# Side products of a three-layer block emitted in batches with a least distance, feeding of operands excepted

## The chip, the cores and the metric

One core of one Trainium2 chip runs the whole program. The metric is the device time of one execution in microseconds; before the change it is 2408.99 us, the median of three runs (2408.96 to 2410.69).

## What is computed

Two blocks follow each other on a sequence of 256 tokens of width 2048, all in float32. The first has two layers of the same form (cut):

```python
h = x @ w_in                                       # split into 11 parts
y_a = chunk_band_attention(a_q, a_k, a_v, table)   # 8 heads of 128, chunks of 64
o_b = gla_chunk_recurrence(b_q, b_k, b_v, log_g)   # 4 heads, gated linear attention, normed
y_m = memory_attention(m_q, *split(mem @ w_mem_kv))  # 4 heads
y = concat([y_a * silu(a_z), y_b * silu(b_z), y_m * silu(m_z)])
x = layer_norm(ALPHA * x + y @ w_out)
```

The second block has one layer:

```python
proj = rms_norm(x) @ w_in                          # a_q a_f a_i a_g b_q b_k b_v b_f g_a g_b
y_a = hgrn2_mixer(a_q, a_f, a_i, a_g) @ w_up_a     # 8 heads: gated recurrence over chunks of 64
y_b = fox_mixer(b_q, b_k, b_v, b_f) @ w_up_b       # 8 heads: causal softmax with decays
x = x + rms_norm((sigmoid(g_a) * y_a + sigmoid(g_b) * y_b) @ w_o)
gate, up = split(rms_norm(x) @ w_ffn_in)           # 5632 each
x = x + rms_norm((silu(gate) * up) @ w_ffn_down)
```

## The kernel before

Nearly all of TensorE's time goes into the large products with the weight matrices. They are a list of jobs, in the order in which they run (`run`, line 212). A job makes 512 output columns (or two jobs of 256, where the output is wanted with features on the partitions) over all rows of the weight; its weight comes in tiles of 128 x 1024 numbers. Each number is split into a high and a low part in the reduced float type that TensorE multiplies fast: ScalarE casts the high part (line 271) and VectorE subtracts it (line 272), and three matmuls (lines 329 to 331) or two (lines 338 and 339) use the parts. One tile is a unit. Its loads (SP's queue) and splits are emitted ahead, up to six split tiles and four raw ones, as far as the 41 slots of SBUF that all stages share allow (`ahead`, `room`). When a job's last unit is emitted, its `post` reads the result out of PSUM.

The small products (scores, transposes, read-outs of attention and recurrence heads, transposes of operands) are side work. A head is a Python generator that emits some instructions, yields a delay and is continued later. A planner keeps a clock in nanoseconds: a unit adds 2623, a side product 1.69 per column. A generator is due when its delay has passed on that clock. After each unit `pump` (line 194) continues the two that have been due longest. A bank is one of four PSUM buffers of 512 columns for side products (`bank`). Tokens allow three recurrence heads and three attention heads at a time. `drain` (line 199) continues given generators until they end, whatever their delay; a `post` or a read of an operand calls it where it needs the result.

Nothing is reordered later: each engine runs its instructions in the order in which they were emitted.

The generators that matter here:

- `hgrn_head` (line 751), one for each of 8 heads in the second block, and for each of two halves t of the sequence: `decay_levels` (line 666: eleven GpSimd instructions, then Abs and Exp of 128 x 1024 on ScalarE, lines 684 and 685), delay 10000; fifteen multiplies on GpSimd (lines 765 to 771), 7500; score products of four levels into one bank and a masked read-out on VectorE (line 781), 3500; the same for four more levels, 3500; for the second half the product with the first half's keys (the cross product), a sum over levels on VectorE (line 784), 5500; the read-out into a bank, its squares on ScalarE (line 691), the power on GpSimd (line 446) and the scaling on VectorE (line 693), 9000; a transpose, 0.
- `banded` (line 602), the softmax heads of both blocks (f heads in the second): scores, bias and maximum on VectorE, exponentials on ScalarE (line 615), scaling on VectorE (line 618), 7000; transposes and a copy by ScalarE (line 623), 8000; the product with the values.
- `post_f` (line 1229), the post of the gate columns f0 and f1, each in two halves: a copy by ScalarE (line 471), two passes of VectorE (lines 472 and 483), two sigmoids (lines 1237 and 1238), three passes of GpSimd (lines 1242 to 1244).
- `post_ag` (line 1339), the post of the output gate's columns: its first half drains the four recurrence heads of the group, and both halves end in a GpSimd multiply (line 812).
- `feeder` and `late_feed` (lines 457 and 529), which transpose and split the operand of the next jobs.

Of the kernel before, what the change touches and what calls it, by code (L numbers as in the profile page):

```python
# [32 lines left out]
NEAR = 8  # L33
HOLD = 4
N_WARM = 12


L0 = 11000
L1 = 7000
F0 = 4500  # L40
F1 = 5500
FG = 1250
# [54 lines left out]
class Builder:  # L97
    def __init__(self, ctx, tc, a):
        self.tc, self.nc, self.a = tc, tc.nc, a
        pool = lambda name, bufs, **kw: ctx.enter_context(tc.tile_pool(name=name, bufs=bufs, **kw))  # L100
        self.const = pool("const", 1)
        self.tmp = pool("tmp", 2)
        self.small = pool("small", 4)
        self.psm = pool("psm", 2, space=bass.MemoryType.PSUM)
        self.pss = pool("pss", 4, space=bass.MemoryType.PSUM)
        self.dram = pool("dram", 1, space=bass.MemoryType.DRAM)
        self.free = list(range(N_SLOT))
        self.act = self.const.tile([P, NKT, 2, S], F32R, tag="act", name="act")
        self.slots = [self.const.tile([P, 1024], F32, tag=f"slot{i}", name=f"slot_{i}") for i in range(N_SLOT)]
        self.side, self.ready, self.pending = [], {}, []  # L110
        self.tokens = {"att": N_ATT, "lin": N_LIN}
        self.clock = 0.0
        self.n = 0


# [28 lines left out]
        return self.tmp.tile(shape, F32, tag=tag, name=self.name(tag), bufs=bufs)  # L144

    def bank(self):
        return self.pss.tile([P, 512], F32, tag="bank", name=self.name("bank"))

    def load(self, out, in_):
        self.nc.sync.dma_start(out, in_)  # L150


    def start(self, gen):
        self.side.append(gen)
        self.ready[gen] = self.clock

    def later(self, fn, delay=1500):
# [34 lines left out]
        self.tokens[kind] -= 1  # L192

    def pump(self):
        due = [g for g in self.side if self.ready[g] <= self.clock]
        for gen in sorted(due, key=lambda g: self.ready[g])[:2]:
            self.step(gen)

    def drain(self, gens):
        tries = 0  # L200
# [179 lines left out]
def network(ctx, tc, a):  # L380
    B = Builder(ctx, tc, a)
# [75 lines left out]
    def feeder(act, t, delay, gap=1500):  # L457
        yield delay
        while act.left[t]:
            act.feed_next(t)  # L460
            yield gap
# [97 lines left out]
    late = {}  # L559

    def start_late(act, *args):
        late["gen"] = late_feed(act, *args)
        B.start(late["gen"])

    def need_rows(act):

# [254 lines left out]
    def memory_jobs(l, act, pre_v=None, pre_k=None, after=None):  # L821
        jobs.append(Job("x", a["w_mem_kv"][l], 512, 512, act, keep_x(mv, l), pre=pre_v))
        wjobs(a["w_mem_kv"][l], 0, act, keep(mk, l, then=after), pre=pre_k)
# [19 lines left out]

    def start_x():
        load_x()
        B.start(first_x())

    def first_x():
        yield 8000
        x_head["ids"] = B.alloc(2, F32R)  # L850
        slot_split(x_head["ids"], v4(x_in[0]))
        B.release([x_in.pop(0)])

    mem_act = Act(main_get, feed_mem, quads, both=True)

    def mem_start():
        load_mem(1)

        def rest():
            for c in (2, 3):  # L860
                load_mem(c)
                mem_act.feed_next(0)
                yield 2000
            B.load(ident, a["c_ident"])
            mem_act.feed_next(0)
        B.start(rest())

    (mem_in[0],) = B.alloc(1)
    mem_act.left[0].pop(0)
# [7 lines left out]
    (load_a, split_a), (load_b, split_b) = mem_half(0), mem_half(1)  # L877
    load_a()
    split_a()
    memory_jobs(0, mem_act, mem_start, start_x, lambda: B.start(feeder(x0, 0, 0)))  # L880

    def head_get(ids):

# [33 lines left out]
    def layer(l, act, head):  # L917
# [126 lines left out]
        def early():  # L1044
            B.release(head())
            for _ in range(3):
                yact.feed_next(0)
            B.start(feeder(yact, 0, 1000))

        W(3584, act, post_z(1, "A1", early), pre=y_head)  # L1050

# [27 lines left out]
        def finish(t):  # L1079
# [7 lines left out]
            if l == 0:  # L1087
                def norm():
                    xsrc["ids"] = st["r"]
                    yield L0 * t  # L1090
                    for c in range(4):
                        V.scalar_tensor_tensor(rows(c), rows(c), mvt[:, 0:1], st["g"](c), ALU.subtract, ALU.mult)
                        V.scalar_tensor_tensor(rows(c), rows(c), rs[:, 0:1], st["bb"](c), ALU.mult, ALU.add)
                    for c in range(4):
                        nc.gpsimd.dma_start(xres[t * P:(t + 1) * P, c * 512:(c + 1) * 512], rows(c))
                    yield from feeder(nact, t, L1)
                    if t == 1:
                        B.release(st["gi"] + st["bi"] + st["head"])
                B.start(norm())
                return  # L1100


# [18 lines left out]

            st[t] = rows, center, stretch, shift
            if t == 0:
                B.start(feeder(nact, 0, F0, FG))
                return

            B.release(st["gi"] + st["wi"])
# [363 lines left out]
    def mix_done(ids, t):  # L1491
        if t == 0:
            xsrc["ids"] = B.alloc(4)

        def rows(c):
            return vt(ids[c])[:, t, :]

        for c in range(4):
            eng = V if c % 2 == 0 else G
            eng.tensor_tensor(vt(xsrc["ids"][c])[:, t, :], rows(c), f["wb"](c), ALU.mult)  # L1500

        f[t] = rows
        if t == 0:
            B.start(feeder(fact, 0, F0, FG))
        else:
            start_late(fact, [f[0], f[1]], x1res, None, lambda: B.release(ids + f["wi"]), False)

# [138 lines left out]
```

## Time and profile before

| | |
|---|---|
| median of 3 runs | 2408.99 us (2408.96 to 2410.69) |
| the profiled execution | 2409.21 us, of it span 2407.4 us |
| mean granted clock of TensorE | 0.998 |
| TensorE busy (matmuls) | 2391.0 us, 99%, 12105 matmuls |
| VectorE busy | 1471.4 us, 61% |
| ScalarE busy | 1098.7 us, 46% |
| GpSimd busy | 399.6 us, 17% |
| DMA | 464.65 MB, mean 193 GB/s |

PE is TensorE's matmuls, PEld its weight loads, DVE VectorE, ACT ScalarE, POOL GpSimd, SP the engine that issues most DMAs. Matmuls are pipelined: the time of one in a row is longer than the distance to the next, so distances of starts are to be read, not durations.

### The profile page before, as it was taken

What the parts mean: (1) busy time and instruction counts of PE and PEld (TensorE: products, weight loads), DVE (VectorE), ACT (ScalarE), POOL (GpSimd) and SP (SyncE); (2) the same over time, 40 slices, a digit from 0 to 9 for tenths busy, and PEclk for the clock granted to TensorE, in tenths of its full rate; (3) what the DMA queues carried; (4) which work ended last, traced back from release to release, by engine and by line L of the source; (5) the groups of instructions that cost most, each with busy time, mean ns of one, the idle gap of its engine ahead of it and who ended that gap; (6) DMA issues with size and microseconds to landing.
All of it is one profiled execution on the core that took longest, in us unless ns stands there. A gap on an engine that the chain in (4) does not pass through costs nothing.

```text
span 2407.4 us, 31457 instructions
## 1 busy us (share of the span) xinstructions
PE 2391.0 (99%) x12105; PEld 2015.4 (84%) x12105; DVE 1471.4 (61%) x1671; ACT 1098.7 (46%) x1472; POOL 399.6 (17%) x601
## 2 busy tenths in 40 slices
PE   9999999999999999999999999999999999999998
PEld 7888888888888888888888888887888888888886
DVE  6587557666855667766675656657545544554455
ACT  5444445345454553555545444445434423443333
POOL 0330010004400110364654430001000000000000
PEclk9999999999999999999999999999999999999999
DMA  9646567674656674954554666675755655555653
GB/s 325 186 149 184 171 188 262 207 241 133 186 159 188 205 258 154 279 166 124 178 164 143 200 190 193 201 243 180 243 176 181 194 184 192 203 182 177 208 193 131
DMA packets 313911, 464.65 MB, mean 193 GB/s; under 512 B 21960, under 2 KB 161568, under 8 KB 313760
## 3 DMA queue, kind: packets, MB, share of 16 engines
q1 hardware_dynamic: 312528, 459.48, 60.3%
q8 instruction: 95, 1.56, 0.3%
q0 software_dynamic: 640, 2.10, 0.2%
q10 hardware_dynamic: 592, 1.06, 0.1%
q14 instruction: 56, 0.46, 0.1%
HBM read 454.18 MB, written 8.40 MB: 192 GB/s over the span
## 4 chain that ended last, share of the span: by engine, by line
PE 91%; issue 6%; DVE 1%; ACT 0%; DMA 0%; POOL 0%; SPq 0%; DVEq 0%; POOLq 0%
PE main_j L338 19%; PE main_j L329 19%; PE main_j L330 19%; PE main_j L331 19%; PE main_j L339 10%; PE bank L372 4%; PE bank L376 1%; PE main_j L334 0%; DMA slot<-in_memT_dram 0%; DVE slot L1480 0%; DVE slot L272 0%; SPq L150 0%; POOL slot L673 0%; ACT slot L271 0%; POOL slot L812 0%
## 5 line engine op out<-in xcount | busy, mean ns | idle before, releaser
L272 DVE TENSOR_TENSOR slot<-slot,slot 128x1024 fp32r<-128x1024 f32 x810 | 1003.0, 1284 | 200.2 <-ACT slot L271 196.5
L271 ACT CAST slot<-slot 128x1024 fp32r<-128x1024 f32 x810 | 807.5, 1047 | 254.9 <-DVE slot L272 129.0
L338 PE MATMUL main_j<-act,slot 128*128 128x512 f32 x1824 | 651.3, 400 | 0.0
L329 PE MATMUL main_j<-slot,act 128*128 128x512 f32 x1608 | 635.6, 395 | 0.6 <-ACT slot L271 0.6
L330 PE MATMUL main_j<-slot,act 128*128 128x512 f32 x1608 | 626.5, 390 | 1.4 <-DVE slot L272 1.2
L331 PE MATMUL main_j<-slot,act 128*128 128x512 f32 x1608 | 626.8, 390 | 0.0
L339 PE MATMUL main_j<-act,slot 128*128 128x256 f32 x1824 | 510.6, 280 | 0.0
L338 PEld LDWEIGHTS main_j<-act,slot 128*128 128x128 f32 x1824 | 343.0, 188 | 80.5 <-issue 1.1
L331 PEld LDWEIGHTS main_j<-slot,act 128*128 128x128 f32 x1608 | 301.8, 188 | 63.7
L330 PEld LDWEIGHTS main_j<-slot,act 128*128 128x128 f32 x1608 | 302.2, 188 | 62.8 <-DVE slot L272 2.2
L329 PEld LDWEIGHTS main_j<-slot,act 128*128 128x128 f32 x1608 | 302.1, 188 | 62.1 <-ACT slot L271 1.1
L339 PEld LDWEIGHTS main_j<-act,slot 128*128 128x128 f32 x1824 | 344.9, 189 | 0.8
L329 PE MATMUL main_j<-slot,slot 128*128 128x512 f32 x600 | 236.3, 394 | 0.0
L331 PE MATMUL main_j<-slot,slot 128*128 128x512 f32 x600 | 233.8, 390 | 0.0
L330 PE MATMUL main_j<-slot,slot 128*128 128x512 f32 x600 | 233.6, 389 | 0.0
L446 POOL TENSOR_TENSOR rsl<-rsl,nhalf 128x1 f32<-128x1 f32 x8 | 6.2, 774 | 993.9 <-DVE rsl L445 993.9
L331 PEld LDWEIGHTS main_j<-slot,slot 128*128 128x128 f32 x600 | 112.6, 188 | 23.9
L329 PEld LDWEIGHTS main_j<-slot,slot 128*128 128x128 f32 x600 | 112.7, 188 | 22.8
L330 PEld LDWEIGHTS main_j<-slot,slot 128*128 128x128 f32 x600 | 112.7, 188 | 22.4
L673 POOL TENSOR_TENSOR slot<-slot 128x128 f32<-128x128 f32 x144 | 82.0, 601 | 202.7 <-PE main_j L338 93.0
L353 ACT CAST slot<-bank 128x512 fp32r<-128x512 f32 (+1 forms) x30 | 15.8, 528 | 175.8 <-PE bank L376 170.1
L812 POOL TENSOR_TENSOR slot<-slot,tz 128x512 f32<-128x512 f32 x20 | 25.9, 1295 | 397.0 <-DVE tz L811 387.2
(193 smaller groups left out, 1730.9 us busy)
## 6 DMA issues: line engine op xcount, KB each, us to landing
slot<-in_w_in_dram SPq DMA_DIRECT2D x384, 512.0 KB, 4.1
slot<-in_w_ffn_in_dram SPq DMA_DIRECT2D x176, 512.0 KB, 4.5
slot<-in_w_ffn_down_dram SPq DMA_DIRECT2D x88, 512.0 KB, 4.7
slot<-in_w_out_dram SPq DMA_DIRECT2D x64, 512.0 KB, 4.5
slot<-in_w_o_dram SPq DMA_DIRECT2D x32, 512.0 KB, 4.7
slot<-in_w_mem_kv_dram SPq DMA_DIRECT2D x31, 512.0 KB, 6.2
slot<-in_w_up_b_dram SPq DMA_DIRECT2D x16, 512.0 KB, 4.2
slot<-in_w_up_a_dram SPq DMA_DIRECT2D x16, 512.0 KB, 3.9
```

The costliest lines, as they stand in the source:

```text
L271: nc.scalar.copy(h, src)
L272: nc.vector.tensor_tensor(l, src, h.bitcast(F32), ALU.subtract)
L329: nc.tensor.matmul(o, xh[:, rows], h[:, k, :], start=st, stop=False)
L330: nc.tensor.matmul(o, xh[:, rows], l[:, k, :], start=False, stop=False)
L331: nc.tensor.matmul(o, xl[:, rows], h[:, k, :], start=False, stop=en)
L338: nc.tensor.matmul(job.ps[:, f, :], h[:, k, fs], xs, start=st, stop=False)
L339: nc.tensor.matmul(job.ps[:, f, :S], l[:, k, fs], xh, start=False, stop=en)
L353: nc.scalar.copy(h, src)
L372: self.b.nc.tensor.matmul(out, *args, **kw)
L376: self.b.nc.tensor.transpose(out, *args)
L673: G.tensor_tensor(view(E[:, l, :]), view(bt), ref, ALU.subtract)
L812: G.tensor_tensor(y, y, tz, ALU.mult)
```

## The change

`pump` no longer continues two generators after each unit. It returns unless something is due and either the clock has reached `self.batch` or one of the due generators is marked urgent. Then it continues the due generators in the order of their ready times, stops when more than two banks have been taken, and sets the next batch to 7000 behind the clock. `bank` counts. `start` gets a flag that marks a generator as urgent, and the generators that load, split or transpose operands of the jobs set it (eight calls). Delays, tokens, drains and jobs are as before.

```diff
+BATCH = 7000
@@
-        self.clock = 0.0
+        self.clock = self.batch = 0.0
+        self.banks, self.urgent = 0, set()
@@
     def bank(self):
+        self.banks += 1
         return self.pss.tile([P, 512], F32, tag="bank", name=self.name("bank"))
@@
-    def start(self, gen):
+    def start(self, gen, urgent=False):
         self.side.append(gen)
+        if urgent:
+            self.urgent.add(gen)
         self.ready[gen] = self.clock
@@
     def pump(self):
         due = [g for g in self.side if self.ready[g] <= self.clock]
-        for gen in sorted(due, key=lambda g: self.ready[g])[:2]:
+        if not due or (self.clock < self.batch and not any(g in self.urgent for g in due)):
+            return
+        banks = self.banks
+        for gen in sorted(due, key=lambda g: self.ready[g]):
+            if self.banks - banks > 2:
+                break
             self.step(gen)
+        self.batch = self.clock + BATCH
@@
-        B.start(late["gen"])
+        B.start(late["gen"], True)
...
-            B.start(feeder(yact, 0, 1000))
+            B.start(feeder(yact, 0, 1000), True)
...
-            B.start(feeder(fact, 0, F0, FG))
+            B.start(feeder(fact, 0, F0, FG), True)
```

## Rows read from the trace of the kernel before

**Rows 1.** The page: TensorE's granted clock in 40 slices of the span.

```profile
PEclk9999999999999999999999999999999999999999
```

**Rows 2.** Timeline around four transposes: start, us, engine, line, operation, count, idle before.

```profile
1851.00 0.39 PE L331 MATMUL main_j<-slot,slot 128*128 128x512 f32 x1
...
1851.23 0.60 PE L376 MATMUL bank<-ident,slot 128*128 128x128 f32 x4
...
1851.58 0.48 PE L329 MATMUL main_j<-slot,slot 128*128 128x512 f32 x1
...
1851.90 0.39 PE L330 MATMUL main_j<-slot,slot 128*128 128x512 f32 x1
...
1852.54 0.69 DVE L354 TENSOR_TENSOR slot<-bank,slot 128x512 fp32r<-128x512 f32 x1 [2.87 <-ACT slot L353]
```

**Rows 3.** Windows: busy us by engine, then granted clock, DMA share, GB/s.

```profile
1130.00:1134.00 4.00, 1.90 (x13) 1.45 (x12) 1.98 (x7) 3.97 (x10) 3.13 (x3) 1.00 0.21 74
1134.00:1138.00 4.00, 4.00 (x16) 3.42 (x15) 3.32 (x6) 3.35 (x5) 3.09 (x6) 0.58 0.46 132
...
1652.00:1656.00 4.00, 2.56 (x15) 1.86 (x15) 4.00 (x5) 2.15 (x4) 2.10 (x2) 1.00 0.90 330
```

**Rows 4.** Timeline of TensorE: score products and transposes of two f heads.

```profile
1120.50 0.92 PE L372 MATMUL bank<-slot,slot 128*128 128x128 f32 x4
...
1130.75 0.49 PE L376 MATMUL bank<-ident,P 128*128 128x128 f32 x3
1133.34 0.70 PE L376 MATMUL bank<-ident,P 128*128 128x128 f32 x3 [2.10 <-DVE P L618]
```

**Rows 5.** Windows of GpSimd alone: a head's multiplies, then a decay.

```profile
1101.00:1110.40 9.40, 9.38 (x16) 1.00 0.41 116
1110.40:1113.80 3.40, 3.40 (x11) 1.00 0.45 144
```

**Rows 6.** Timeline of ScalarE: a decay's Abs, a table load.

```profile
1113.83 1.06 ACT L684 ACTIVATE slot<-slot 128x1024 f32<-128x1024 f32 x1 [7.47 <-POOL slot L683]
...
1130.29 1.28 ACT L615 ACT_TABLE_LOAD   x1
```

**Rows 7.** The page's groups: the weight split; last columns are busy us, mean ns, idle before.

```profile
L272 DVE TENSOR_TENSOR slot<-slot,slot 128x1024 fp32r<-128x1024 f32 x810 | 1003.0, 1284 | 200.2 <-ACT slot L271 196.5
L271 ACT CAST slot<-slot 128x1024 fp32r<-128x1024 f32 x810 | 807.5, 1047 | 254.9 <-DVE slot L272 129.0
```

**Rows 8.** Timeline: a post of the gate columns, first copy, split, sigmoid, last pass.

```profile
1126.09 0.58 ACT L471 COPY slot<-main_j 128x512 f32<-128x512 f32 x1
...
1126.55 1.21 DVE L272 TENSOR_TENSOR slot<-slot,slot 128x1024 fp32r<-128x1024 f32 x1
...
1132.16 1.04 POOL L1244 TENSOR_TENSOR slot<-slot,om 128x512 f32<-128x512 f32 x1
```

**Rows 9.** Timeline of VectorE: first and last of an f head's softmax.

```profile
1129.01 0.34 DVE L1320 SCALAR_TENSOR_TENSOR P<-slot,ct,slot 128x128 f32<-128x128 f32 x1
...
1132.81 0.74 DVE L618 TENSOR_SCALAR P<-P,rc 128x128 f32<-128x128 f32 x2
```

**Rows 10.** Last head's transpose, second step behind; output gate's posts (ns, first and last).

```profile
1458.84 0.27 PE L376 MATMUL bank<-ident,sc 128*128 128x128 f32 x1
...
1459.18 0.40 PE L330 MATMUL main_j<-slot,act 128*128 128x512 f32 x1
...
L812 POOL TENSOR_TENSOR slot<-slot,tz x4: 1280/1284/1287, 1476.7 to 1510.6; 128x512 f32<-128x512 f32 x4
```

**Rows 11.** Timeline: a head's read-out and its scaling.

```profile
1447.48 0.38 PE L372 MATMUL bank<-slot,sc 128*128 128x128 f32 x2
...
1449.34 0.29 DVE L693 TENSOR_TENSOR sc<-bank,rs 128x128 f32<-128x128 f32 x1 [0.66 <-POOL rs L446]
```

**Rows 12.** Timeline of VectorE: masked score read-out, sum over levels.

```profile
1429.60 0.69 DVE L781 TENSOR_TENSOR slot<-bank,slot 128x512 f32<-128x512 f32 x1 [2.76 <-PE bank L372]
...
1442.53 2.03 DVE L784 TENSOR_REDUCE sc<-slot 128x128 f32<-128x1024 f32 x1
```

More of the change, by code (lines that the diff above doesn't have):

```diff
@@ L845, in start_x @@
         load_x()
-        B.start(first_x())
+        B.start(first_x(), True)
     def first_x():
@@ L865, in rest @@
             mem_act.feed_next(0)
-        B.start(rest())
+        B.start(rest(), True)
     (mem_in[0],) = B.alloc(1)
@@ L879, in network @@
     split_a()
-    memory_jobs(0, mem_act, mem_start, start_x, lambda: B.start(feeder(x0, 0, 0)))
+    memory_jobs(0, mem_act, mem_start, start_x, lambda: B.start(feeder(x0, 0, 0), True))
     def head_get(ids):
@@ L1098, in norm @@
                         B.release(st["gi"] + st["bi"] + st["head"])
-                B.start(norm())
+                B.start(norm(), True)
                 return
@@ L1123, in finish @@
             if t == 0:
-                B.start(feeder(nact, 0, F0, FG))
+                B.start(feeder(nact, 0, F0, FG), True)
                 return
```

## Prediction, made before the result was known

> **What bounds the kernel now.** I read the page first. The granted clock stands at nine tenths or more in all forty slices of the span [rows 1]. TensorE is busy in 99% of it: main products stand back to back, a step of 512 columns every 0.23 us, and the side products (scores, transposes, read-outs of the heads) are put between them. So only three things can move the time: what a change from main to side products costs, TensorE's stalls, and its clock.
>
> The change of work is nearly free. From the first of four transposes to the second main step behind them is 0.67 us [rows 2], and from a single transpose to the second main step 0.34 [rows 10]. So three transposes more cost 0.33, 0.11 each. With that and a main step of 0.23 both sums close: at most 0.01 us is left for the two changes together, although the first main step behind looks long (0.32). Its surplus is the last transpose's own time, which its row doesn't show.
>
> The stalls are few. The longest that a side product causes is at 1133 us: the transposes of a softmax wait 2.10 us for VectorE's scaled probabilities (step of 2.59 us where 0.33 is due, so 2.26 lost) [rows 4]. Behind it the clock falls: mean 0.58 in the next 4 us [rows 3], that is 4 x 0.42, about 1.6 us of work lost. The cause is order, not load: ScalarE is idle 7.47 us, held by the Abs of a decay whose inputs GpSimd hadn't made [rows 6]. GpSimd was busy with 9.4 us of a head's multiplies and then 3.4 us of the decay itself [rows 5]. ScalarE, VectorE and GpSimd each go through their instructions in the order of emission, so this decay held up the weight splits and the softmax behind it.
>
> **The change, part by part.** The planner's clock decides the order. A unit of main work (one weight tile) is 2.62 us on it (2.8 us of TensorE). Before, each unit is followed by up to two due steps. Now a batch opens when 7 us have passed on that clock since the end of the last one, and takes due steps until three banks are used (a step of two banks may make it four). I followed that clock through the code with every delay, bank, slot and token; for the code of before this gives the order of side products that the trace shows.
>
> *Fewer changes of work.* 204 runs of side products become 147. 57 x 0.01 us = 0.5 us saved. Between nothing and, if the whole surplus of 0.09 us in the first main step were a price, 5 us. I take 0.5, since the two runs of [rows 2, 10] leave no more.
>
> *Urgent feeders.* The flagged generators open a batch at once, and their steps fall on the same planner marks as before, as do the loads issued with them on SP's queue. Cost nothing. The cover is that few other steps are due in those stages; with three banks used ahead of it, a feed would come one unit (2.8 us) later.
>
> *Longer lives of slots.* Side steps end later, so free slots run down, and tiles split ahead fall from 6 to 3 or 4 in parts of the first block. Three tiles are still 8 us of main work against a split of 1.05 on ScalarE and 1.28 on VectorE [rows 7]. Nothing; up to 3 us if a blocked ScalarE falls on it.
>
> *The second block's first batches (f heads).* Here the mechanism of 1113 us gets worse, since a batch puts decay and softmax next to each other. On the planner's clock: 1084.3 first half of the gate column f1 ends (its post is a copy on ScalarE, two passes on VectorE, two sigmoids, three GpSimd passes); 1086.9 batch with a decay, then the score products of both f heads; 1096.3 second half of f1 ends, same post; 1096.5 batch with a head's read-out, a decay, then both f heads' transposes; 1105.7 the f heads' outputs. In TensorE's time from the first end: the three GpSimd passes are done at 6.2 (7.1 from copy to last pass, less a split of some 1.2 that stood in between [rows 8]). The decay is behind them in GpSimd's order: 9.6 [rows 5]. ScalarE's two passes of 1.06 and a load of the exponential's table of 1.28 [rows 6]: 13.0. Then the softmax: a head's chain is 4.5 us from first pass to last [rows 9], 3.2 without the table load that stood in it. Of the first head's I leave 2.1, since VectorE's first passes run while ScalarE waits: 15.1. The second's stands behind the first's scaling in VectorE's order: 18.3. TensorE is there at 2.8 + 1.45 (score products, a transpose) + 3 x 2.8 + 0.2 = 12.9. It waits 2.2 and then 2.9, together 5. Bounds: 1 (ScalarE gets at the decay early) to 8 (decay of 5 us).
>
> From 18.6 TensorE needs three units and wants the copied transposes at 27. ScalarE and VectorE first do three splits (to 22.1 on VectorE), then f1's second post (VectorE 1.4, sigmoids 1.2; GpSimd to 27.6), the read-out's power (0.6), the decay (3.4), its two passes and the table load again (3.4), the copy (0.5): 35.5. That is a wait of 8.5. It is 0 if the splits and the post stand early enough for ScalarE to keep up. I take 5, nearer to the upper end, since the row of 1113 us shows that one decay behind a multiply alone holds ScalarE 7.5 us.
>
> Each of these two stalls is as long as the one of 2.1 us that the clock followed, so 2 x 1.6 for the clock (0 to 3.4). The stall of today in the same place is replaced: 2.26 + 1.6 = 3.9 back.
>
> *The last heads of the recurrence.* A half of a head is seven steps with delays of 10, 7.5, 3.5, 3.5, 5.5, 9 and 0 us. Rounded up to batches 8 to 11 us apart, they take 8 or 9 batches where units were waited for before. Before, the last head's transpose is at 1458.8, while the column whose post drains these heads ends some 35 us later (four posts from 1476.7 to 1510.6, the third counts) [rows 10]. Now, on the planner's clock, the last head has its multiplies at 1436.9 and the drain comes at 1439.7, with seven steps open: one head's read-out and transpose, and for the other both score halves, the cross product, the read-out and the transpose. They are emitted with no main product between. TensorE then waits for each link. Read-out to normalized rows is 2.2 us from the read-out's start (1447.48 to 1449.63) [rows 11], less its own 0.44: 1.8. The first time the other head's scores (0.9) lie in it: 0.9. From the second score half to the read-out: mask pass 0.69 and sum 2.03 [rows 12], 2.8 with the hand-overs. So 0.9 + 2.8 + 1.8 = 5.5. The multiplies (9.4 us [rows 5]) start behind the output pass of the column before (1.28 [rows 10]) and may be late for the first scores: 0 to 4, I take 1. Clock: 1.6 (0 to 2). Sum 8, between 5 and 12.
>
> The Trainium skill ("TensorE: Matmul & The Clock Gate", "Why this matters for your kernels") says that idle gaps between bursts of matmuls send the clock back to half. The trace agrees once (1134 us) and differs once: the wait of 1.6 us at 1652 left it at 1.00 [rows 3]. By that rule each of the three places pays; without any fall the forecast would be 4.8 us lower.
>
> *Elsewhere.* Drains in the first block find only an empty last step open. In the feed-forward part one transpose group is drained one unit before use: 2.0 us to its split's end (1851.23 to 1853.23) [rows 2] against 3.2 us of TensorE's own work. Nothing, up to 1.
>
> **Sum.** The profiled execution's own time 2409.2 (0.2 over the median of the runs) + 5 + 5 + 3.2 + 8 - 3.9 - 0.5 = 2426.0; on the median 2425.8. Forecast 2426 us, 0.7% slower.
>
> **The rivals.**
> *Only the drain costs.* If VectorE and ScalarE keep up in the f heads as now, the old stall stays and nothing is added: 2409.2 + 8 - 0.5 = 2416.7. For it: ScalarE is busy 46% on the whole. Against: the order of the instructions is fixed, and idle engines don't help behind a wait.
> *Spacing cures the stalls (not slower).* Every step now stands at least as far from the one before as its delay asks, so softmaxes are ready when TensorE comes: the stall and clock fall of 1133 us go (-3.9), fewer changes (-0.5), and the drain, whose pieces of idle are split up, pays 5.5 without the clock: 2410.3. It decides at the f heads' transposes: if ScalarE passes the decay before 11 us instead of 13.0, with the second head's chain overlapped. For it: 10 us lie between scores and transposes. Against: they lay that far apart before too, at 1120.5 and 1133.3 less the wait [rows 4].
> *Everything at its upper end.* GpSimd's passes run at the slow end of what the rows show, and the drain's multiplies are late: 8 + 8.5 + 3.4 + 12 - 4.4 = +27.5, 2436.7.
> *Changes of work have the price* of 0.09 us: 57 x 0.09 = 5 us off the forecast, 2421; against it the closed sum.
>
> **How the numbers follow.** The forecast 0.58 (with the price of changes in it), only the drain 0.2, spacing cures 0.12, upper end 0.1. The range 2411 to 2438 takes in all but the low half of the curing case and what lies over the upper end; the forecast's own range is 2419 to 2433. What a measurement can tell from no change is about 0.2%, 4.8 us: up to 2413.8. Slower 0.84: the forecast, the upper end and 0.16 of the drain alone (the rest of that case, a short drain of 5 us, is within). Same 0.12, from that rest and two thirds of the curing case. Faster 0.04, the remainder, where the drain too finds its links done.
>
> **What would show it.** Right: transposes of the f heads waiting for VectorE, and their outputs for ScalarE, with ScalarE idle before Abs; a row of side products without main products between them just before the third output column's post, with waits for VectorE's sum and the normalized rows; clock at half behind these. Wrong: no wait of TensorE over 2 us in either place; a shorter step of main products behind side products; new waits for weight tiles in the first block, where I count nothing.

## The result, and the profile after

The changed kernel takes **2443.03 us** (median of 4 runs, 2442.49 to 2444.21) against 2409.79 for the kernel before in the same session (4 runs, 2408.96 to 2410.69): a ratio of 1.0140, 95% interval 1.0128 to 1.0152. It is slower, as forecast (2426), but by twice as much: 33 us instead of 17, and above the range's upper end of 2438. The profiled span grew from 2407.4 to 2441.7 us, by 34.3.

To see where, take the start of the same main product in both traces, after minus before, place by place, less the side products that one kernel has done by then and the other hasn't (0.11 us for a record of 128 columns, half of it where two 64-row products run beside each other). A difference that stays constant over a stretch means that nothing is lost in it:

| place (us in the changed kernel) | lost | the prediction's term |
|---|---|---|
| first block, to 1053 | 4.5 | 0 (longer lives of slots, up to 3), and -0.5 for fewer changes of work |
| start of the second block's attention, 1053 to 1094 | 6.0 | 0 |
| f heads of the second block, 1094 to 1195 | 13.1 | 5 + 5 + 3.2 - 3.9 = 9.3 |
| drain of the last recurrence heads, 1504 to 1544 | 11.9 | 8 |
| between them, and the rest | -1.2 | 0 |
| sum | 34.3 | 16.8 |

The slices of the granted clock still show 9 everywhere, as in [rows 1], since a slice is 61 us long. In the page's part 2 of the changed kernel the row of busy TensorE has one new dent, in the slice from 1465 to 1526 us:

```profile
PE   9999999999999999999999998999999999999998
...
PEclk9999999999999999999999999999999999999999
```

The list of TensorE's waits by what ended them (sum in us, times, longest) names the places; the kernel before had one long entry in them, the 2.10 of [rows 4]:

```profile
PE bank L389 <- DVE P L631: 6.0, 3, 3.8
PE bank L385 <- ACT P L636: 5.6, 1, 5.6
PE bank L385 <- DVE sc L797: 4.6, 2, 2.6
PE bank L389 <- DVE sc L706: 3.6, 2, 1.9
PE main_j L351 <- ACT slot L284: 2.3, 1, 2.3
```

Lines stand 13 later than in the kernel before: L389 are the transposes, L385 the other side products, L631 the softmax's scaling, L636 the copy of its transposes, L797 the sum over levels, L706 the scaling of a head's read-out, L351 a main product that wants a weight tile, L284 and L285 the two passes of a weight split.

**The f heads** went as the prediction wrote it out. TensorE's rows (start, duration, idle before in brackets) answer to [rows 4]:

```profile
1145.92 0.95 PE L389 MATMUL bank<-ident,P 128*128 128x128 f32 x3 [3.85 <-DVE P L631]
1148.90 0.95 PE L389 MATMUL bank<-ident,P 128*128 128x128 f32 x3 [2.03 <-DVE P L631]
...
1165.81 2.93 PE L385 MATMUL bank<-P,slot 128*128 128x128 f32 x12 [5.57 <-ACT P L636]
```

Behind them is, twice, a wait of ScalarE like the one in [rows 6], here with the gate post's passes of [rows 8] in front of the decay instead of a head's multiplies: GpSimd takes the last of the three passes (L1257) and then the decay (L686 to L696), and ScalarE's Abs (L697) stands still until that is done. GpSimd's rows, then ScalarE's, each of the first time and of the second:

```profile
1135.39 2.02 POOL L1257 TENSOR_TENSOR slot<-slot,om 128x512 f32<-128x512 f32 x1
1137.37 2.44 POOL L686 TENSOR_TENSOR slot<-slot 128x128 f32<-128x128 f32 x6
...
1156.98 1.04 POOL L1257 TENSOR_TENSOR slot<-slot,om 128x512 f32<-128x512 f32 x1
```
```profile
1141.05 1.06 ACT L697 ACTIVATE slot<-slot 128x1024 f32<-128x1024 f32 x1 [6.40 <-POOL slot L696]
...
1161.97 1.06 ACT L697 ACTIVATE slot<-slot 128x1024 f32<-128x1024 f32 x1 [6.41 <-POOL slot L696]
1163.04 1.28 ACT L698 ACT_TABLE_LOAD   x1
1164.33 1.06 ACT L698 ACTIVATE slot<-slot 128x1024 f32<-128x1024 f32 x1
1165.30 0.84 ACT L636 COPY P<-bank 128x384 f32<-128x384 f32 x2
```

**The drain** has four waits and no main product between 1515.5 and 1528.3. The first wait was not foreseen: the sum (L797) of the head that is further along is late too, since VectorE does three weight splits ahead of it. TensorE, then VectorE:

```profile
1517.85 0.49 PE L385 MATMUL bank<-slot,sc 128*128 128x128 f32 x2 [2.07 <-DVE sc L797]
...
1521.36 0.30 PE L389 MATMUL bank<-ident,sc 128*128 128x128 f32 x1 [1.91 <-DVE sc L706]
...
1525.34 0.77 PE L385 MATMUL bank<-slot,sc 128*128 128x128 f32 x2 [2.56 <-DVE sc L797]
...
1528.22 0.45 PE L389 MATMUL bank<-ident,sc 128*128 128x128 f32 x1 [1.69 <-DVE sc L706]
```
```profile
1510.91 4.32 DVE L285 TENSOR_TENSOR slot<-slot,slot 128x1024 fp32r<-128x1024 f32 x3
...
1515.92 1.87 DVE L797 TENSOR_REDUCE sc<-slot 128x128 f32<-128x1024 f32 x1
```

**The start of the second block's attention** is the place that the prediction priced at nothing. A weight tile is late, because ScalarE waited 6.40 us for VectorE's pass over the forget gate's rows (L1302), then went through that step's exponential and logarithm, and then through a decay's (L697, L698), which the same batch had emitted. Only then came the next splits. Before, those two steps stood in different units. ScalarE's rows, VectorE's and TensorE's:

```profile
1056.12 0.51 ACT L1303 ACTIVATE slot<-slot,bf 8x256 f32<-8x256 f32 x1 [6.40 <-DVE slot L1302]
...
1061.42 1.06 ACT L697 ACTIVATE slot<-slot 128x1024 f32<-128x1024 f32 x1 [2.16 <-DVE slot L1306]
...
1064.75 2.92 ACT L284 CAST slot<-slot 128x1024 fp32r<-128x1024 f32 x3
```
```profile
1047.38 5.93 DVE L285 TENSOR_TENSOR slot<-slot,slot 128x1024 fp32r<-128x1024 f32 x2 [6.66 <-ACT slot L284]
...
1055.68 0.41 DVE L1302 TENSOR_TENSOR slot<-bank,rbc 8x256 f32<-8x256 f32 x1
```
```profile
1065.83 0.80 PE L351 MATMUL main_j<-act,slot 128*128 128x512 f32 x1 [2.34 <-ACT slot L284]
```

VectorE's two splits at 1047.38 took 5.93 us beside a head's multiplies on GpSimd; two at 1065.81 took 2.52, also beside a head's multiplies, and there it was the multiplies that were long (up to 1.34 us each, against 0.31 at 1048). With 2.52 at the first place too, L1302 would by this estimate have come 3.4 us earlier, which is more than the 2.34 that the tile was late. So the long splits look as necessary for this wait as the order of the steps.

**The clock** fell in each of these places. The windows (busy us by engine, then the granted clock; [rows 3] are those of before) show it at half of 2.4 GHz, which is 1.2, where they give 0.51, and partly so in the others. The last line is the wait that [rows 3] show at 1652, 1.44 us idle, with the clock at 1.00 in both kernels:

```profile
1063.20:1072.10 8.90, 6.09 (x19) 4.28 (x17) 6.25 (x6) 7.79 (x9) 7.11 (x10) 0.63 0.38 106
1141.00:1149.50 8.50, 2.62 (x14) 1.78 (x13) 3.21 (x14) 6.54 (x13) 0.01 (x1) 0.68 0.36 113
1149.50:1154.30 4.80, 4.80 (x17) 4.12 (x16) 4.58 (x5) 3.57 (x5) 0.00 (x0) 0.51 0.00 0
1160.00:1171.30 11.30, 5.73 (x23) 5.10 (x22) 4.19 (x5) 8.57 (x11) 11.30 (x29) 0.70 0.04 16
1515.00:1526.40 11.40, 4.86 (x32) 4.02 (x30) 7.80 (x10) 0.63 (x3) 5.89 (x14) 0.85 0.72 219
1526.40:1533.20 6.80, 5.11 (x17) 4.33 (x17) 3.96 (x7) 3.62 (x7) 1.83 (x2) 0.51 0.37 132
1684.00:1690.00 6.00, 4.56 (x23) 3.56 (x22) 5.86 (x6) 1.36 (x4) 3.20 (x3) 1.00 0.93 320
```

### The profile page after: what moved, and what is told of

Read it like the earlier page. It is cut to its first block, busy times and chain, and to the rows that moved or that the text cites. A ratio compares the mean times of both kernels' runs of the same rounds, so it can differ in the third digit from the quotient of the medians.

```text
span 2441.7 us, 31404 instructions
## 1 busy us (share of the span) xinstructions
PE 2404.6 (98%) x12105; PEld 2024.6 (83%) x12105; DVE 1474.3 (60%) x1671; ACT 1099.1 (45%) x1472; POOL 394.9 (16%) x601
## 3 DMA queue, kind: packets, MB, share of 16 engines
q8 instruction: 95, 1.56, 0.3%
## 4 chain that ended last, share of the span: by engine, by line
PE 48%; issue 8%; POOL 2%; DVE 2%; ACT 1%; DMA 0%; DVEq 0%; POOLq 0%; ACTq 0%; SPq 0%
PE main_j L344 13%; PE main_j L343 13%; PE main_j L342 13%; PE main_j L351 4%; PE main_j L352 2%; PE bank L385 2%; PE bank L389 1%; DVE slot L285 1%; POOL slot L686 1%; DVE slot L1125 0%; POOL slot L778 0%; DMA slot<-in_ln_g_dram 0%; POOL slot L779 0%; DVE slot L1493 0%; ACT L698 0%
## 5 line engine op out<-in xcount | busy, mean ns | idle before, releaser
L285 DVE TENSOR_TENSOR slot<-slot,slot 128x1024 fp32r<-128x1024 f32 x810 | 1003.1, 1287 | 162.3 <-ACT slot L284 157.3
L284 ACT CAST slot<-slot 128x1024 fp32r<-128x1024 f32 x810 | 806.4, 1047 | 268.3 <-DVE slot L285 107.8
L351 PE MATMUL main_j<-act,slot 128*128 128x512 f32 x1824 | 657.0, 403 | 2.3 <-ACT slot L284 2.3
L342 PE MATMUL main_j<-slot,act 128*128 128x512 f32 x1608 | 632.6, 393 | 1.0 <-ACT slot L284 0.7
L351 PEld LDWEIGHTS main_j<-act,slot 128*128 128x128 f32 x1824 | 346.6, 190 | 86.0 <-ACT slot L284 2.7
L342 PEld LDWEIGHTS main_j<-slot,act 128*128 128x128 f32 x1608 | 302.0, 188 | 63.4 <-ACT slot L284 1.1
L342 PE MATMUL main_j<-slot,slot 128*128 128x512 f32 x600 | 235.5, 393 | 0.0
L342 PEld LDWEIGHTS main_j<-slot,slot 128*128 128x128 f32 x600 | 112.7, 188 | 22.9
L686 POOL TENSOR_TENSOR slot<-slot 128x128 f32<-128x128 f32 x144 | 81.7, 599 | 241.0 <-PE main_j L351 160.3
L459 POOL TENSOR_TENSOR rs<-rs,nhalf 128x1 f32<-128x1 f32 (+1 forms) x26 | 16.1, 619 | 400.3 <-DVE rs L458 394.8
```

What stands on the lines that cost most here:

```text
L284: nc.scalar.copy(h, src)
L285: nc.vector.tensor_tensor(l, src, h.bitcast(F32), ALU.subtract)
L342: nc.tensor.matmul(o, xh[:, rows], h[:, k, :], start=st, stop=False)
L351: nc.tensor.matmul(job.ps[:, f, :], h[:, k, fs], xs, start=st, stop=False)
L459: G.tensor_tensor(out, out, nhalf[:, :n], ALU.pow)
L686: G.tensor_tensor(view(E[:, l, :]), view(bt), ref, ALU.subtract)
```

## The experiments

Twelve kernels, each the changed kernel with one edit unless it says otherwise. Ratios are to the kernel before, run beside them (its medians 2409.24, 2409.09 and 2409.51).

**e1: the old order in the second block's attention.** From the start of that attention to its second output-gate column, the planner picks as before (cut: the lines that set `old`):

```diff
     def pump(self):
         due = [g for g in self.side if self.ready[g] <= self.clock]
+        if self.old:
+            for gen in sorted(due, key=lambda g: self.ready[g])[:2]:
+                self.step(gen)
+            return
```

> The changed kernel, but from the start of the second block's attention until its second output-gate column's splits the planner takes up to two due steps after every unit, as before; batches everywhere else. Theory (the loss of 34 us sits in three places of that attention part, where an order of instructions makes TensorE wait and its clock falls; the batches of the first block cost 4.4 of it and those of the feed-forward part nothing): 2410 + 4.4, about 2414 us (2412 to 2417), clock at 1.00 except the one stretch at the place where the kernel before has it. Rival (the least distance and the joined runs of side products cost a little everywhere, and the stalls are only where it shows): 2425 us or more.

Measured 2412.73 us, ratio 1.0015 (1.0005 to 1.0024). All but 3.5 of the 33 us come from that one part of the program; the rival with a cost everywhere falls. The one wait of before is there again, but this time no fall of the clock followed it. The wait (lines stand 5 later here than in the changed kernel: L636 is the softmax's scaling), and a window around:

```profile
PE bank L394 <- DVE P L636: 2.1, 1, 2.1
```
```profile
1130.00:1146.00 16.00, 13.78 (x85) 11.77 (x84) 13.09 (x23) 12.46 (x22) 10.48 (x15) 1.00 0.47 133
```

**e2: the last recurrence heads urgent**, so that they don't wait for batches:

```diff
             if c == 3:
                 B.release(st["yb0"] + st["yb1"])
+                B.urgent.update(gens["h1"])
```

> The changed kernel, but the last recurrence heads (of h1) are made urgent once the fourth up-projection column's post has run, so that their open steps no longer wait for a batch. Theory (the drain's 11.9 us come only from seven linked steps standing open when the third output column's post drains them; with the heads urgent one step is open): the waits at 1515 to 1533 us go and the clock stays at 1.00 there; 2443 - 11.9, about 2431 us (2429 to 2434). The other places stay as they are: waits of 2.3 for a weight tile, 3.9 and 2.0 for the f heads' transposes, 5.6 for their outputs. Rival (the links are late because GpSimd's multiplies and VectorE's sums are, so the waits only move ahead to the same steps between main products): 2439 us or more, with waits of 1 us and over for VectorE's sums before 1515 us.

Measured 2431.17 us, ratio 1.0091 (1.0076 to 1.0106): 11.9 less, as expected. No wait for a head's sum or scaling is left in its list of waits, and the clock is at 1.00 there. The drain's price is that of steps left open, not of slow links.

**e3: the forget gate's rows not beside the decay:** `B.start(gens["bf"], True)`.

> The changed kernel, but the generator of the forget-gate rows (bf), started at the second block's beginning, is urgent: it opens its own batch instead of sharing one with the first recurrence head's decay. Theory (the wait of 2.34 us for a weight tile at 1063 us and the 6.8 us at half clock behind it come from these two side steps' posts standing together on ScalarE and VectorE): the wait and the fall of the clock at 1063 to 1072 us go; 2443 - 6.0, about 2437 us (2434 to 2440) if the batches behind it fall as they do now. Rival (VectorE's split is stretched by GpSimd's multiplies wherever bf stands, and the tile is late anyway): the wait at 1063 us stays over 1.5 us and the time at 2443.

Measured 2437.49 us, ratio 1.0117 (1.0102 to 1.0132). The number is the theory's, but only half of it for the theory's reason. The wait at 1063 us and its fall of the clock are gone (5 us less by 1094; 1.00 from 1060 to 1075), so the two steps had to stand together for it. The long splits went with it (three at 1052.94 took 3.50 us), so the share of order alone and that of the splits are not told apart. The condition, that the batches behind fall as they did, did not hold: the f heads' three waits went too, and others came, so that the sum is near the expected one by chance (L498 is the scaling of a projection's columns):

```profile
PE bank L385 <- DVE sc L797: 7.7, 3, 3.0
PE bank L389 <- DVE sc L706: 5.5, 2, 3.8
PE bank L385 <- DVE slot L498: 5.0, 1, 5.0
```
```profile
1060.00:1075.00 15.00, 15.00 (x90) 13.12 (x89) 9.59 (x11) 10.24 (x13) 11.66 (x16) 1.00 0.58 182
```

**e4: the three gate passes on VectorE:** `G.tensor_tensor` becomes `V.tensor_tensor` in the lines L1255 to L1257.

> The changed kernel, but the three passes that turn the forget column's two sigmoids into the gate and the key (two multiplies and an addition) run on VectorE instead of GpSimd; the arithmetic is the same. Theory (the f heads' waits come from GpSimd's order: those passes, then a decay behind them, which holds ScalarE's Abs for 6.4 us twice and the softmax behind it): the decay is done about 4 us earlier each time, the transposes' waits (3.9 and 2.0) and the outputs' wait (5.6) shrink by as much, to under 2 in sum of each, most of the clock's fall goes; about 2433 us (2430 to 2437). Rival (VectorE is the late one: it has the splits and two softmaxes in front, and three more passes make it later): the transposes still wait 4 us or more in sum, 2443 us or above.

Measured 2434.27 us, ratio 1.0106 (1.0089 to 1.0123): 8.8 less. Half of the theory held: the transposes' waits went. The outputs' wait grew to 6.73 us. GpSimd's decay now begins behind a read-out's power, which waits for VectorE, and VectorE has the three passes in front; ScalarE's Abs still stands 5.40 us for it, and the copy behind that Abs:

```profile
1150.61 0.57 POOL L459 TENSOR_TENSOR rs<-rs,nhalf 128x1 f32<-128x1 f32 x1 [18.79 <-DVE rs L458]
...
1154.10 0.45 POOL L696 TENSOR_SCALAR slot<-slot 128x64 f32<-128x64 f32 x1
```
```profile
1154.58 1.06 ACT L697 ACTIVATE slot<-slot 128x1024 f32<-128x1024 f32 x1 [5.40 <-POOL slot L696]
```

**e10: the copy off ScalarE as well**, for the f heads alone: `A.copy(pt[:, :384], tb[:, :384])` becomes `V.tensor_copy(...)`.

> The changed kernel with the three gate passes on VectorE, and the copy of the f heads' transposes on VectorE too instead of ScalarE, where it stood behind the second decay's Abs. Theory (with the passes moved the transposes' waits went, and the outputs' wait of 6.7 us that was left is the copy's place behind that Abs in ScalarE's order; the splits stand behind the Abs as well, but three tiles split ahead, 8.4 us of main products, cover them): no wait of the f heads over 1 us, 2443 - 13.5, about 2429 us (2428 to 2432). Rival (the splits behind the same Abs are the next late thing, or VectorE with a copy more is): a wait of 2 us or more for a weight tile or for VectorE between 1150 and 1172 us, 2432 to 2437 us.

Measured 2429.15 us, ratio 1.0080 (1.0063 to 1.0096): 13.9 less. The longest wait of the f heads is 0.33 us, the clock from 1141 to 1173 is 1.00, and what the rival named came only as 1.56 us for a weight tile, at 1161.6. So both stalls came from ScalarE's order behind a decay, as traced: the first went when the decay came earlier (e4), the second when the copy left ScalarE.

**e12: e10 and e2 together.**

> The two edits for the f heads (gate passes and copy on VectorE) and the urgent last recurrence heads together, on the changed kernel. Theory (the places are separate and their costs add): 2443 - 13.5 - 12, about 2418 us (2416 to 2421), of which 6 us over the kernel before are the wait for a weight tile at 1063 us and 3.5 the first block. Rival (the urgent steps push others, as moving the forget rows' step did, and a new wait takes a good part of the gain): 2424 us or more.

Measured 2416.48 us, ratio 1.0029 (1.0018 to 1.0040): the two places add (13.9 + 11.9 = 25.8; 26.6 measured). What is left over the kernel before is the weight tile's wait at 1063 us, the first block and some 3 us around a new wait of 1.93 us for a weight tile at 1161, less before's own stall (3.9 us with its clock), which is not there either. None of the twelve beats the kernel before.

**e7, e9: what the clock costs.** Products that nobody reads fill the waits, in the waiting step's own bank (cut: the table `COVER` of how many for which bank):

```diff
     def bank(self):
         self.banks += 1
+        tile = self.pss.tile([P, 512], F32, tag="bank", name=self.name("bank"))
+        for _ in range(COVER.get(self.banks, 0)):
+            self.nc.tensor.matmul(tile[:, :P], self.ident, self.ident, start=True, stop=True)
+        return tile
```

> The changed kernel with products that nobody reads put into the waits: identity times identity, 128 columns each, in the bank of the waiting step ahead of its first product, 30, 16 and 48 of them before the f heads' two groups of transposes and the first output, and 16, 14, 20 and 12 before the four waiting steps of the drain. They are a little shorter than each wait (0.11 us each against 3.9, 2.0, 5.6, 2.1, 1.9, 2.6 and 1.7 us), so TensorE has work and the side steps start when they did. Theory (behind each place the clock falls because TensorE stood idle, and that costs some 6 us of main products and up to 1.5 us of side products on top of the idle time): the granted clock stays at 1.00 in 1141 to 1171 and 1515 to 1533 us, 2443 - 6 to 7.5, about 2436 us (2435 to 2439); the stretch at 1063 to 1072 stays. Rival (the slow stretches are not set by this idle time, or cost nothing because TensorE waits there anyway): the clock falls as before and the time is 2442 us or more.

> The experiment with products that nobody reads in the seven waits, with half as many, since its trace showed two records of 0.11 us for each such product and so covers twice as long as meant: now 16, 8 and 23 before the f heads' transposes and the first output, and 8, 7, 10 and 6 in the drain (3.5, 1.7, 5.0 and 1.7, 1.5, 2.2, 1.3 us against waits of 3.9, 2.0, 5.6 and 2.1, 1.9, 2.6, 1.7). Theory (the slow stretches behind the f heads and the drain cost about 6 us of main products and up to 1.5 of side products beside the idle time): no fall of the clock there, 2443 - 6 to 7.5, about 2436 us (2435 to 2439). Rival (the falls cost nothing that TensorE would not have waited for): 2442 us or more.

e7 took 2448.54 us, ratio 1.0163 (1.0149 to 1.0177). I had taken a record's 0.11 us for a product's; a product has two records, the covers were twice too long, and its time says nothing. Its clock does: 1.00 in both places. e9, with the right length, took 2438.84 us, ratio 1.0118 (1.0103 to 1.0133), 4.2 less than the changed kernel (5.2 less at the two places by the traces). That is within the theory's range, at its far end, and less than the 6 to 7.5 that the theory gave; the rival's 2442 is out: the falls follow TensorE's idleness and cost about 5 us. Some of what the clock gives back goes into the next wait: the f heads' outputs still wait 2.2 us behind 5.0 us of covers, 7.2 where the changed kernel waited 5.57, since TensorE arrives earlier for the same copy. In the second group of transposes the covers themselves waited 1.13 us for their bank. Windows of the changed kernel, then of e9:

```profile
1141.00:1173.00 32.00, 20.56 (x93) 17.41 (x92) 14.12 (x27) 20.03 (x32) 18.07 (x40) 0.73 0.21 64
1513.00:1533.00 20.00, 11.77 (x59) 9.88 (x58) 13.57 (x18) 5.26 (x12) 9.59 (x17) 0.75 0.60 184
```
```profile
1141.00:1173.00 32.00, 28.39 (x201) 25.86 (x200) 13.64 (x27) 21.38 (x34) 18.07 (x41) 1.00 0.22 66
1513.00:1531.00 18.00, 16.69 (x124) 15.23 (x123) 12.29 (x16) 5.07 (x11) 7.40 (x16) 1.00 0.65 200
```

**e5: three banks without a distance:** `BATCH = 0`.

> The changed kernel with the least distance set to nothing: after every unit a batch of due steps runs until three banks are used, where the kernel before took at most two steps. Followed through the code, no drain then finds more than an empty last step, and the two f heads' transposes of the second block stand ahead of the gate column's post that blocked them. Theory (the least distance makes the whole loss; steps joined into one run cost what they cost apart): the stall of before goes (3.9 us), nothing comes, 2406 us, between 2404 and 2411. Rival (steps that stand joined in one run cost more than the same steps apart, as 4.4 us in the first block of the changed kernel seem to say): 2414 us or more, with the first block alone 3 us or more longer than before.

Measured 2424.16 us, ratio 1.0060 (1.0047 to 1.0073). Both sides missed. The first block loses nothing (-0.1 us at 738, -0.3 at 1030), so joined steps as such are free, against the rival; but the second block's attention loses 15 us without any distance, against the theory. The stall of before went and others came, three of them long:

```profile
PE bank L385 <- DVE slot L498: 5.6, 2, 3.9
PE bank L385 <- DVE sc L797: 2.7, 2, 1.9
```

Those are 7.5 us (1.67, 1.94 and 3.89); the rest, in waits under 1.1 us and in products at the lower clock, I did not place. It may be that the limit of two steps in a unit had done part of the spacing that this attention's queues need; no run shows it.

**e6: no urgent feeders:** the two lines that mark a generator urgent are taken out.

> The changed kernel without its second half: generators that feed operands are not marked urgent and wait for a batch like the others. Followed through the code, ten feeds then come only when a main product wants them. Theory (the marks do what they say and cost nothing; without them TensorE waits at each of these for its transposes' split, 2.0 us from the first transpose to the split's end as in rows 2, with the clock at half behind most): ten waits of 1 to 2.5 us, 2443 + 10 x 2 to 3.5, about 2465 us (2455 to 2480). Rival (the feeds are wanted late enough, or their operands ready early enough, that the marks make no difference): 2440 to 2447 us.

Measured 2481.80 us, ratio 1.0300 (1.0286 to 1.0314): 38.8 us more, over the theory's 22. The marks are needed; the waits are fewer and longer than I took them for (lines stand 2 earlier here: L342 is a main product that wants the low part of its operand, L383 the side products, here with the norm's factors):

```profile
PE main_j L342 <- DVE act L365: 14.5, 3, 7.3
PE bank L383 <- DVE gw L559: 11.9, 1, 11.9
```

**e8: the kernel before, with the gate passes on VectorE.**

> The kernel before, with the three passes that turn the forget column's sigmoids into gate and key on VectorE instead of GpSimd. Theory (before's one long stall, 2.1 us for the f heads' transposes and the fall of the clock behind it, comes from GpSimd's order, as the same waits went in the changed kernel): 2410 - 3.9, about 2406 us (2404 to 2408). Rival (VectorE is the later engine there, or another wait comes in its place): 2409 to 2412 us.

Measured 2411.27 us, ratio 1.0007 (0.9998 to 1.0016): the rival. The second softmax stands behind the three passes in VectorE's order, and the transposes wait longer than the 2.10 of [rows 4]:

```profile
1136.70 0.70 PE L376 MATMUL bank<-ident,P 128*128 128x128 f32 x3 [3.36 <-DVE P L618]
```

**e11: runs of 64-row products broken.** The first block's score products have 64 rows and run two beside each other. A run costs more than its pairs; here a 128-row product is put between pairs, 48 times:

```diff
                 for l in range(4 * half, 4 * half + 4):
+                    if l % 4:
+                        nc.tensor.matmul(banks[0][:, l % 4, :], ident, ident, start=True, stop=True)
                     for e, ps in enumerate(halves):
```

> The changed kernel with 48 products that nobody reads (identity times identity, 128 rows, 0.22 us each) put between the pairs of 64-row score products of the first block's recurrence heads, three in each half-step, so that 48 runs of 64-row products are broken in two. Theory (what the first block lost are changes between 64-row and 128-row products: a run of 16 such pairs takes 2.18 us where pairs 0.11 us apart make 1.78, so 0.4 us for each run's two changes, and the changed kernel has 7 such runs in a layer where the kernel before has 5): 48 x (0.22 + 0.4) = 30 us more, about 2473 us (2468 to 2477). Rival (the surplus around a run belongs to its length or its place, a change of rows itself costs nothing): 48 x 0.22 = 10 us more, about 2453 us.

Measured 2472.38 us, ratio 1.0258 (1.0238 to 1.0279), 29.4 more; the theory. Each break costs 0.4 us beside its product. In the trace a round of four 64-row records (0.22) and one product (0.22) takes 0.84. Where the rows change, the load of the weights (PEld) starts together with its product; where 128 rows follow 128 rows it starts ahead, as in the kernel before, whose row of weight loads is last and belongs to the transposes at 1851.23 in [rows 2]:

```profile
122.51 0.49 PE L385 MATMUL bank<-slot,slot 64*128 64x128 f32 x4
122.93 0.30 PEld L740 LDWEIGHTS bank<-ident 128*128 128x128 f32 x2
122.93 0.49 PE L740 MATMUL bank<-ident 128*128 128x128 f32 x2
123.35 0.49 PE L385 MATMUL bank<-slot,slot 64*128 64x128 f32 x4
```
```profile
1851.00 0.58 PEld L376 LDWEIGHTS bank<-ident,slot 128*128 128x128 f32 x4
```

The Trainium skill ("TensorEngine Tiling (Array Packing)", "Key Properties") says that changing the tiling mode drains TensorE. The trace agrees: a load that doesn't start ahead, and 0.4 us for the change there and back.

## Why the prediction was wrong

**What held.** The direction, both places that it named, and the chains in them: decay behind the gate passes, ScalarE held by its Abs, softmax and copy behind that (e4 and e10 take them apart), and the drain of open steps (e2). The stall of before was replaced. Neither "spacing cures" nor "only the drain" came, and even "everything at its upper end" (2436.7) fell short, since it kept two places at nothing. "Changes of work have the price" would have made the changed kernel faster than forecast.

**Step "longer lives of slots: nothing; up to 3 us if a blocked ScalarE falls on it".** This failed, and it is the largest single miss: at the start of the second block's attention, for which the sum had no term, a blocked ScalarE did fall on it, and 6.0 us were lost at 1053 to 1094. Without them the changed kernel would have taken about 2437 us, inside the range. I looked for late tiles by counting tiles split ahead, and three were enough in the first block. In the second block ScalarE is held not by its own load but by its order, for 6.40 and then 2.16 us, and the work of both steps stands in front of the next splits; that is the kind of wait I wrote out for the f heads, and I did not follow it through the first batches of that attention. e3 shows that the two steps standing together caused it; how much the long splits beside GpSimd's multiplies added stays open.

**Step "longer lives of slots / fewer changes of work": 0 and -0.5.** The first block lost 4.5 in the trace, 3.5 by e1. I priced a change between main and side products on rows of 128-row products [rows 2, 10], where it is free, and took that for all. The 64-row runs pay 0.4 us each, and batching splits them: 7 runs in a layer instead of 5, in two layers, 4 x 0.4 = 1.6 us. e11 shows the price, and e5, whose first block has the 5 runs of before, loses nothing there. The other 2 to 3 us are in pieces of under 0.3 us and stay open.

**Terms "transposes +5" and "outputs +5".** The waits were 3.85 + 2.03 = 5.9 and 5.57, nearly as worked out, yet 9.3 became 13.1: 13.1 + 3.9 - 11.45 leaves 5.5 us for the slow clock, where I had 3.2. e9 takes only 2.6 of it back, because the rest returns as waiting: with TensorE kept busy the outputs' wait comes to 7.2, and in e4 it is 6.73. At full clock the 8.5 that I had worked out and then cut to 5 was nearer; in the changed kernel the slow clock hid the difference.

**Term "drain +8".** Idle 8.2 us against 5.5 and 1: the wait for the sum of the head further along, 2.07, was missed. I had taken that sum as done when the drain came and not asked what VectorE had in front of it: three splits, 4.32 us. The 1 for late multiplies did not come; no wait names GpSimd.

**Term "clock 4.8".** Near what keeping TensorE busy gave back in its two places: 4.2 by e9's median, 5.2 by the traces (2.6 and 2.7). What these places lost beyond their idle time is twice it, 5.5 and 11.9 - 8.2 = 3.7; in the f heads most of the rest comes back as waiting, in the drain 1 us stays open. The fall behind the late weight tile comes on top, within the 6.0. The rule of the Trainium skill that I weighed ("TensorE: Matmul & The Clock Gate", "Why this matters for your kernels"), that idle gaps between bursts send the clock back to half, is borne out where it was tested: filling the gaps kept 1.00. The page gives it for gaps above a length, which the prediction left out, so the fall at 1134 us is no test of the page. The rule as I used it is not enough to foresee one fall: 2.10 us of the same wait was followed by half clock in the kernel before [rows 3] and by 1.00 in e1. The wait at 1652 that I gave as 1.6 us is 1.44.

**The reading of before's stall.** I laid the 2.10 us at 1133 to the decay that held ScalarE 7.47 us at 1113.8. That is not what stood in front of it. ScalarE was idle again for 4.43 us before the first softmax's exponentials at 1123.79, and the second's, at 1131.59, stood behind the gate column's two sigmoids and two table loads of 1.28 us each. In e5 a decay holds ScalarE longer (8.17 us at 1108.33), the gate post stands behind both softmaxes, and their transposes wait for nothing. By these rows it was the gate post in front of the softmax, and e8 fits: three more passes of that post on VectorE made the wait longer. No run moves the post alone.

**Step "urgent feeders cost nothing".** Nothing in the changed kernel contradicts it; e6 shows that without the marks 39 us more would be lost.

## What to carry to other kernels

Where engines work through their instructions in the order of emission, price a new order at every place where two steps come to stand side by side, not at the place where the old order was already tight: follow what each engine has in front of the one thing that TensorE wants, weight splits included. A spacing rule for one engine is an order for all of them, and one step moved into a batch of its own can shift all behind it (e3), so a local mend is measured on the whole. A step that is forced open by a drain pays for each of its links.

## What was not expected of the hardware

A change from 128-row to 64-row products and back costs TensorE 0.4 us (e11: 48 of them, 29.4 us with 0.22 each for the products between), while a change between main and 128-row side products costs nothing that the rows show. The price of a lower clock is partly hidden in front of a wait: 17 us of covers in the waits gave 4.2 us, not the 6 to 7.5 that the slow stretches alone suggested. VectorE's splits and GpSimd's multiplies lengthen each other, and which of them pays changes from place to place: two splits took 5.93 us at 1047 and 2.52 at 1066, while a multiply took 0.31 and up to 1.34.
